# Weights of the first two combined Strassen items ranked ahead of the gate's taps, and no modulation step in them

## The chip, the core and the metric

The kernel runs on one core of a Trainium2 chip. The time is device microseconds of one execution, measured on the core. Three executions of the kernel before took 2934.47, 2937.22 and 2940.39 us, so the median is 2937.22 us. One more execution was profiled; all rows of the profile come from it.

## What is computed

Two layers, each a mixer and a convolutional feed-forward network (FFN), with a modulation of scales and shifts from a condition vector. Layer 0 mixes with a gated delta rule, layer 1 with retention. All in 32-bit floats, sequence 1024, model width 1024, FFN width 2816.

```python
e = silu(c @ cond_w + cond_b)
for i in range(2):
    mod = (e @ ada_w[i] + ada_b[i])[:, None, :]
    sh1, sc1, g1, sh2, sc2, g2 = split(mod, 6)
    y = mixers[i](x * (1.0 + sc1) + sh1)        # gated delta rule, then retention
    x = layer_norm(ALPHA * x + (1.0 + g1) * y, ln_g[i, 0], ln_b[i, 0])
    h = x * (1.0 + sc2) + sh2
    gate, up = split(h @ ffn_up[i], 2)
    gate = causal_dwconv(gate, conv_w[i]) + conv_b[i]   # 3 taps along the sequence
    y = (silu(gate) * up) @ ffn_down[i]
    x = layer_norm(ALPHA * x + (1.0 + g2) * y, ln_g[i, 1], ln_b[i, 1])
```

## The kernel before

**Products.** Every 32-bit operand of a matrix product is split into a high part, a rounded copy that ScalarE writes (line 89), and a low part, the difference that VectorE writes (line 90). `mm3` (lines 110 to 112) issues three matmuls for each pair: weights low by data high, high by low, high by high. The low part can only be made once the high part is there, and the first matmul of a triple needs the low part, so a product starts after its VectorE split.

**The Strassen stage.** `strassen` (from line 1153) computes a product of the transposed activations with weight columns, in *items* of two weight tiles each. It is called three times: for the up projection of the FFN of layer 0 (22 items), for the input projection of retention, and for the FFN of layer 1 (22 items). Items 0 and 1 are done plainly by `side`. From item 2 on an item is *combined*: `wino` does seven half-size products instead of eight, with four weight blocks a11, a12, a21, a22 (one DMA each for a11/a12 and a21/a22). Three of the products need sums of weight blocks, made on VectorE by `psub` (line 1205): s1 = a21 + a22, s2 = s1 - a11, s4 = a12 - s2, s3 = a11 - a21. Each product's weights are split by `block` into a tile `wb`. The products run in this order on TensorE: a11, a12, s1 by T1 (into Z), s2 by T2, s4 by 22, s3 by T3, a22 by T4. The T operands are sums of blocks of activations; `rest()`, called after the first plain item, issues what is left of them. A copy `pc` (line 1225, ScalarE) takes Z out after the product of s1.

In an FFN every even item is a gate item and every odd one the matching half of the up projection. A gate item ends in `conv()`: for each of four tiles one scaled copy on ScalarE (line 1579), two shifted multiply-adds ("taps") on VectorE (line 1584), a SiLU on ScalarE (line 1585). An up item multiplies the gate into it (line 1598), adds blocks on GpSimd (line 1605) and stores the result `o` to memory `ad` (line 1589).

**Modulation steps.** Parts of the modulation are computed bit by bit in the background. `bg` is a list of *units*; `bg_step()` runs the next one. A unit loads 512 KB of `ada_w` (tile `mvw`, line 216, on SyncE's queue) and adds it up in two VectorE instructions (lines 221 and 223, both 223 from the second unit of a group on); every fourth unit ends a group with four transposes on TensorE (line 233), four ScalarE copies (line 235) and a small addition. `wino` takes two steps in each combined item. The FFN of layer 0 has 40 units for its 20 combined items, so its list is empty when the stage ends; the FFN of layer 1 has 8 units; retention has none. While the stage runs, `mvw` tiles come from a spare tag; after it, `bg_tag` is "wr" (line 1265).

**The projection.** `proj_gen` does the down projection after each FFN, also by seven combined products. For layer 0 each product has 11 inner blocks of 12 matmuls. A block's two operands are `ab` (from a raw tile `ar`, read back from `ad`) and `bb` (from `Bw` or `Br`, `ffn_down`); both are split as above. `ab` tiles come in turn from the tags "wl", "hTb" and "wr" (block n from the n mod 3rd), and "wr" has two buffers. Each block calls `bg_step()` once (line 1503), which does nothing if the list is empty:

```python
at = ... ("wl", "hTb", "wr")[n % 3] if early else ...
a = two(at, F32R, "ab")
split(a[0], a[1], ra)
```

**What sets the order.** Each engine runs its instructions in the order of a list. A scheduler writes the lists ahead of time from the program's order as priority and from its own estimates of when operands are there; `tc.high_priority(n)` moves what is issued in it n places up in priority, and `tc.cur_priority` is the place now. A tag's buffers go round, so a tile waits until the last reader of the tile that had its buffer is done. SyncE's queue holds nearly all DMA issues and also runs in order: an issue that waits for a buffer holds all behind it.

Of the kernel before, what the change touches and what calls it, by code (L numbers as in the profile page):

```python
# [12 lines left out]
ALU = mybir.AluOpType  # L13
# [20 lines left out]
def trunk_kernel(ctx: ExitStack, tc, A):  # L34
    nc = tc.nc
    pe, act, dve, pool, sp = nc.tensor, nc.scalar, nc.vector, nc.gpsimd, nc.sync
# [9 lines left out]
    def tl(tag, shape, dt=F32, name=None):  # L46
        return sb.tile(shape, dt, tag=tag, name=name or tag, bufs=BUFS[tag])
# [40 lines left out]
    def split(dst_h, dst_l, src, eng=dve):  # L88
        act.activation(dst_h, src, AF.Copy)  # L89
        eng.tensor_tensor(dst_l, src, dst_h, ALU.subtract)  # L90
# [28 lines left out]
    def bg_step(tile=mm_tile):  # L119
        bg_ps[0] = tile  # L120
        if bg:
            bg.pop(0)()
# [38 lines left out]
    for k in range(KT):  # L161
        w = two("hTa", F32, "mvw")
# [617 lines left out]
    def t_solve(qd_):  # L780
        yield after_ev(("T0", 2 * qd_ - 1), ("A", 2 * qd_), ("A", 2 * qd_ + 1))
        yield from take("lane", 1)
        busy.append(qd_)
        X = tl("lane", [P, 32, 32], name="X")
        for h in pairs[2 * qd_] + pairs[2 * qd_ + 1]:
            for b in range(4):
                bs = slice(32 * b, 32 * b + 32)
                act.activation(X[bs, :, h % 4 * 8:h % 4 * 8 + 8].rearrange("p i c -> p c i"), U[h][bs, :, bs], AF.Copy)
        yield from take("lane", 2)
        yield LAT["X"]  # L790
        Y = tl("lane", [P, 32, 32], name="Y")
        dve.transpose(flat(Y), flat(X))
        T = tl("lane", [P, 32, 32], name="T")
# [210 lines left out]
    def tail(p, h, q4):  # L1004
# [3 lines left out]
        act.activation(d, o, AF.Square)  # L1008
        dve.tensor_reduce(so, d, AX.X, ALU.add)
        dve.scalar_tensor_tensor(so, so, 1.0 / P, ssq[h][:, qs], ALU.mult, ALU.add)  # L1010
# [82 lines left out]

    LAT = {"kk": 3.05, "ld": 1.14, "g1": 17.30, "gm": 2.50, "mm": 1.81, "T": 4.98, "X": 3.38, "fs": 2.2, "T0": 5.00, "t1": 1.65, "t2": 2.35, "t3": 1.34, "D": 2.67, "s1": 1.60, "s2": 1.22, "s3": 1.26, "tail": 12.31, "ssq": 9.30, "fv": 2.85}
    pairs = [(2 * p, 2 * p + 1) for p in range(GH // 2)]
# [57 lines left out]
    def strassen(hT0, xts, scale, shift, items, tags=("hTb", "hTb", "qkv", "qkv", "aux"), direct=False, beside=None, spare="lane"):  # L1153
        B = {"11": hT0[:4], "21": hT0[4:]}
        nblk = [0]
        nacc = [0]

        def mm_on(*a, **kw):
            return pe.matmul(*a, skip_group_check=True, **kw)  # L1159

        def side(n, s):
            out = []
            for u in items[n][:2]:
                w = load_w(u)
                X = acc_tile()
                for i, b in enumerate((("11", "21"), ("12", "22"))[s]):
                    for k in range(4):
                        mm3(X, w, k + 4 * i, B[b][k], i == 0 and k == 0, i == 1 and k == 3)
                out.append(X)
            return out  # L1170

        ahead, sinks = [], []
        for n in range(2):
            X = side(n, 0)
            if direct:
                sinks.append(items[n][2]())
                for i in range(2):
                    sinks[n](2 * i, X[i], None)
                continue
            ahead.append([tl("cv", [P, 516], name="ah")[:, 0:HALF] for _ in range(2)])  # L1180
            for t, x in zip(ahead[n], X):
                act.activation(t, x, AF.Copy)
        rest = build_T(B, xts, scale, shift, tags)

        def block(src):
            n = nblk[0]
            nblk[0] += 1
            t = tl(("wh", "wl")[n % 2], [P, 2, HALF], F32R, name="wb")
            split(t[:, 0], t[:, 1], src)
            return kn(t[:, 0]), kn(t[:, 1])  # L1190

        def prod(src, b, onto=None):
            w = block(src)
            if onto is None:
                nacc[0] += 1
                acc = (acc_tile, acc_tile, sc_tile)[nacc[0] % 3]()
            else:
                acc = onto
            for k in range(4):
                mm3(acc, w, k, B[b][k], onto is None and k == 0, k == 3, mm_on if onto is not None else pe.matmul)  # L1200
            return acc

        def psub(x, y, op=ALU.subtract):
            t = mm_tile()
            dve.tensor_tensor(t, x, y, op)  # L1205
            return t

        def wino(n, sink):
            ua, ub = items[n][:2]
            raws = []  # L1210
            for m, u in ((2 * n, ua), (2 * n + 1, ub)):
                if direct and m % 3 == 0:
                    raws += [tl("xT", [P, HALF], name="wr") for _ in range(2)]
                    for h2 in range(2):
                        anchor["i"] = sp.dma_start(raws[-2 + h2], u[:, hs(h2)])
                else:
                    w = tl("wr", [P, D])
                    anchor["i"] = sp.dma_start(w, u)
                    raws += [w[:, hs(0)], w[:, hs(1)]]
            if beside:  # L1220
                beside(n)
            a11, a12, a21, a22 = raws
            def copy_of(X, tag="cv"):
                t = tl(tag, [P, 516] if tag == "cv" else [P, HALF], name="pc")[:, 0:HALF]
                act.activation(t, X, AF.Copy)  # L1225
                return t

            X = prod(a11, "11")
            p1 = copy_of(X)
            s1 = psub(a21, a22, ALU.add)  # L1230
            sink(0, prod(a12, "21"), p1)
            s2 = psub(s1, a11)
            Z = prod(s1, "T1")
            z5 = copy_of(Z)
            s4 = psub(a12, s2)
            prod(s2, "T2", X)
            u2 = copy_of(X)
            s3 = psub(a11, a21)
            prod(s4, "22", Z)
            sink(1, Z, u2)  # L1240
            bg_step()
            prod(s3, "T3", X)
            u3 = copy_of(X, "t2")
            sink(3, X, z5)
            sink(2, prod(a22, "T4"), u3)
            bg_step()

        bg_tag[0] = spare
        for n in range(2):
            if not direct:  # L1250
                sinks.append(items[n][2]())
                for i in range(2):
                    sinks[n](2 * i, ahead[n][i], None)
            X = side(n, 1)
            for i in range(2):
                sinks[n](2 * i + 1, X[i], None)
            if n == 0:
                rest()
            if items[n][3]:
                items[n][3]()  # L1260
        for n in range(2, len(items)):
            wino(n, items[n][2]())
            if items[n][3]:
                items[n][3]()
        bg_tag[0] = "wr"
        return B
# [449 lines left out]
    for t in range(4):  # L1716
        if t % 2 == 0:
            xw = tl("lane", [P, 2, HALF], name="xlo")
        x = xw[:, t % 2]
# [273 lines left out]
```

## Time and profile before

| what | value |
|---|---|
| median of three executions | 2937.22 us (2934.47 to 2940.39) |
| the profiled execution | 2931.49 us |
| its span, first to last instruction | 2929.3 us |
| mean granted TensorE clock | 0.989 of full |
| TensorE busy | 2808.1 us (96%), 13638 matmuls |
| VectorE busy | 2198.4 us (75%) |
| ScalarE busy | 1316.2 us (45%) |
| GpSimd busy | 421.1 us (14%) |

Rows of a timeline read: start in us, duration in us, engine, line, operation, output<-inputs, tile shapes, how many; in brackets the idle time before it and what ended it. A row "xN" stands for N instructions one after the other. The duration of a matmul includes the time in which the next one is already running: at the full clock one starts every 0.227 us. Line numbers in rows are those of the kernel before.

### The profile page before, as it was taken

What the parts mean: (1) busy time and instruction counts of PE and PEld (TensorE: products, weight loads), DVE (VectorE), ACT (ScalarE), POOL (GpSimd) and SP (SyncE); (2) the same over time, 40 slices, a digit from 0 to 9 for tenths busy, and PEclk for the clock granted to TensorE, in tenths of its full rate; (3) what the DMA queues carried; (4) which work ended last, traced back from release to release, by engine and by line L of the source; (5) the groups of instructions that cost most, each with busy time, mean ns of one, the idle gap of its engine ahead of it and who ended that gap; (6) DMA issues with size and microseconds to landing.
All of it is one profiled execution on the core that took longest, in us unless ns stands there. A gap on an engine that the chain in (4) does not pass through costs nothing. (4 is left out here: it accounts for less than half of the span.)

```text
span 2929.3 us, 38823 instructions
## 1 busy us (share of the span) xinstructions
PE 2808.1 (96%) x13638; PEld 2296.3 (78%) x13638; DVE 2198.4 (75%) x3965; ACT 1316.2 (45%) x2457; POOL 421.1 (14%) x485
## 2 busy tenths in 40 slices
PE   8998999999999999999999999999999899999997
PEld 7777877887778888887787877777778688888786
DVE  6695687556788888897687766666697887778888
ACT  3755465443544444536443332221345544444443
POOL 0311220134011111100000000223201011111001
PEclk9999999999999999999999999999999999999999
DMA  8122221354344444863434454555564233335753
GB/s 309 64 80 80 98 91 44 105 187 148 108 150 159 163 157 147 316 218 123 157 110 173 149 181 149 165 172 163 189 235 155 94 137 108 108 108 202 262 158 119
DMA packets 239234, 442.35 MB, mean 151 GB/s; under 512 B 22848, under 2 KB 76352, under 8 KB 239040
## 3 DMA queue, kind: packets, MB, share of 16 engines
q1 hardware_dynamic: 206832, 387.96, 39.4%
q10 hardware_dynamic: 29760, 43.00, 4.0%
q0 software_dynamic: 2448, 8.91, 0.8%
q8 instruction: 107, 1.75, 0.2%
q14 instruction: 87, 0.71, 0.1%
HBM read 331.26 MB, written 108.53 MB: 150 GB/s over the span
## 5 line engine op out<-in xcount | busy, mean ns | idle before, releaser
L1466 PE MATMUL acc<-bb,ab 128*128 128x512 f32 x1800 | 427.5, 393 | 6.5 <-DVE pa L1441 2.5
L1466 PEld LDWEIGHTS acc<-bb,ab 128*128 128x128 f32 x1800 | 338.0, 189 | 81.4 <-DVE bb L90 3.8
L630 PE MATMUL acc<-hT,wh 128*128 128x512 f32 x960 | 300.3, 394 | 0.0
L1605 POOL TENSOR_TENSOR o<-o 128x512 f32<-128x512 f32 x88 | 121.1, 1387 | 810.6 <-DVE o L1598 680.4
L89 ACT ACTIVATE ab<-ar 128x512 fp32r<-128x512 f32 x210 | 129.0, 624 | 184.2 <-PE acc L1466 93.3
L1159 PE MATMUL acc<-T,wb 128*128 128x512 f32 x840 | 204.2, 392 | 7.2 <-DVE wb L90 7.2
L630 PEld LDWEIGHTS acc<-hT,wh 128*128 128x128 f32 x960 | 183.0, 191 | 34.0
L630 PE MATMUL acc<-hT,wl 128*128 128x512 f32 x480 | 202.8, 422 | 0.8 <-DVE qkv L993 0.5
L1159 PEld LDWEIGHTS acc<-T,wb 128*128 128x128 f32 x840 | 157.9, 189 | 43.7 <-DVE wb L90 11.1
L90 DVE TENSOR_TENSOR ab<-ar,ab 128x512 fp32r<-128x512 f32 x210 | 146.4, 703 | 44.2 <-ACT ab L89 44.2
L90 DVE TENSOR_TENSOR wb<-mm,wb 128x512 fp32r<-128x512 f32 x216 | 145.2, 684 | 23.4 <-ACT wb L89 21.7
L90 DVE TENSOR_TENSOR wb<-wr,wb 128x512 fp32r<-128x512 f32 x162 | 111.3, 688 | 65.7 <-ACT wb L89 63.8
L1225 ACT ACTIVATE pc<-acc 128x512 f32<-128x512 f32 x143 | 84.7, 592 | 160.5 <-PE acc L1159 91.6
L89 ACT ACTIVATE wh<-wr 128x1024 fp32r<-128x1024 f32 x101 | 107.0, 1061 | 110.2 <-PE acc L630 50.3
L89 ACT ACTIVATE wb<-mm 128x512 fp32r<-128x512 f32 x216 | 122.3, 593 | 72.8 <-DVE mm L1205 72.1
L90 DVE TENSOR_TENSOR wl<-wr,wh 128x1024 fp32r<-128x1024 f32 x85 | 105.5, 1241 | 61.2 <-ACT wh L89 59.1
L89 ACT ACTIVATE wb<-wr 128x512 fp32r<-128x512 f32 x162 | 99.7, 627 | 96.5 <-DMA wr<-in_ffn_up 53.0
L449 DVE SCALAR_TENSOR_TENSOR qkv<-raw,vc,qkv 128x512 f32<-128x512 f32 x144 | 112.3, 783 | 34.8 <-ACT qkv L447 30.7
L630 PE MATMUL acc<-wh,hT 128*128 128x512 f32 x384 | 135.5, 415 | 0.7 <-DVE vv L90 0.7
L1584 DVE SCALAR_TENSOR_TENSOR o<-g,vc,o 128x512 f32<-128x512 f32 (+2 forms) x176 | 135.2, 786 | 0.7
L223 DVE SCALAR_TENSOR_TENSOR ada<-mvw,e,ada 128x512 f32<-128x512 f32 x140 | 105.9, 757 | 27.0 <-DMA mvw<-in_ada_w 26.5
L110 PE MATMUL acc<-T,wb 128*128 128x512 f32 x292 | 116.6, 399 | 9.9 <-DVE wb L90 9.4
(626 smaller groups left out, 6876.5 us busy)
## 6 DMA issues: line engine op xcount, KB each, us to landing
wr<-in_ffn_up SPq DMA_DIRECT2D x96, 512.0 KB, 4.3
ad<-o SPq DMA_DIRECT2D x154, 256.0 KB, 2.2
ar<-ad SPq DMA_DIRECT2D x154, 256.0 KB, 4.2
mvw<-in_ada_w SPq DMA_DIRECT2D x48, 512.0 KB, 5.5
Br<-in_ffn_down SPq DMA_DIRECT2D x66, 256.0 KB, 3.3
mvw<-in_ada_w SPq DMA_DIRECT2D x64, 256.0 KB, 3.0
wr<-in_ret_wv SPq DMA_DIRECT2D x32, 512.0 KB, 4.2
ar<-od SPq DMA_DIRECT2D x56, 256.0 KB, 5.0
```

Of the source, the lines that this page charges most:

```text
L89: act.activation(dst_h, src, AF.Copy)
L90: eng.tensor_tensor(dst_l, src, dst_h, ALU.subtract)
L110: mm(acc, wl[:, k], hl[0], start=first, stop=False)
L223: dve.scalar_tensor_tensor(a, wr[kk], e[:, k:k + 1], a, ALU.mult, ALU.add)
L449: dve.scalar_tensor_tensor(oh, raw[:, 3 - j:515 - j], w[:, 3 - j:4 - j], oh, ALU.mult, ALU.add)
L630: pq(pe.matmul(out, lhsT, rhs, start=start, stop=stop, **kw), cost)
L1159: return pe.matmul(*a, skip_group_check=True, **kw)
L1225: act.activation(t, X, AF.Copy)
L1466: mm_ = (lambda *a, p=p, onto=onto, **kw: (mm if p < 2 else pe.matmul)(*a, skip_group_check=onto, **kw))
L1584: dve.scalar_tensor_tensor(tv, gv[:, c0 - j:c1 - j], w[:, 2 - j:3 - j], tv, ALU.mult, ALU.add)
L1605: pool.tensor_tensor(o[d], o[x], o[y], op)
```

## The change

`strassen` notes the priority at the point behind `rest()` of the first plain item, ahead of that item's `conv()` (the list `mark`). In items 2 and 3, the first two combined ones, the sums of weights (`psub`) and the splits (`block`) are issued at the priority of that point, by the context manager `rank`. And these two items call no `bg_step()`. The number of units stays, so the four steps that are no longer taken there are taken later: in the FFN of layer 1 in items 4 to 7 instead of 2 to 5; in the FFN of layer 0, where 40 units stood against 40 steps, the last four units are left when the stage ends, and the projection's first product takes them, one at each of its blocks 0 to 3.

```diff
--- before.py
+++ after.py
@@ -1154,6 +1154,7 @@
         B = {"11": hT0[:4], "21": hT0[4:]}
         nblk = [0]
         nacc = [0]
+        mark = []
 
         def mm_on(*a, **kw):
             return pe.matmul(*a, skip_group_check=True, **kw)
@@ -1182,15 +1183,19 @@
                 act.activation(t, x, AF.Copy)
         rest = build_T(B, xts, scale, shift, tags)
 
-        def block(src):
+        def rank(n):
+            return tc.high_priority(tc.cur_priority - mark[0]) if n < 4 else nullcontext()
+
+        def block(src, it):
             n = nblk[0]
             nblk[0] += 1
             t = tl(("wh", "wl")[n % 2], [P, 2, HALF], F32R, name="wb")
-            split(t[:, 0], t[:, 1], src)
+            with rank(it):
+                split(t[:, 0], t[:, 1], src)
             return kn(t[:, 0]), kn(t[:, 1])
 
-        def prod(src, b, onto=None):
-            w = block(src)
+        def prod(it, src, b, onto=None):
+            w = block(src, it)
             if onto is None:
                 nacc[0] += 1
                 acc = (acc_tile, acc_tile, sc_tile)[nacc[0] % 3]()
@@ -1200,9 +1205,10 @@
                 mm3(acc, w, k, B[b][k], onto is None and k == 0, k == 3, mm_on if onto is not None else pe.matmul)
             return acc
 
-        def psub(x, y, op=ALU.subtract):
+        def psub(it, x, y, op=ALU.subtract):
             t = mm_tile()
-            dve.tensor_tensor(t, x, y, op)
+            with rank(it):
+                dve.tensor_tensor(t, x, y, op)
             return t
 
         def wino(n, sink):
@@ -1225,25 +1231,27 @@
                 act.activation(t, X, AF.Copy)
                 return t
 
-            X = prod(a11, "11")
+            X = prod(n, a11, "11")
             p1 = copy_of(X)
-            s1 = psub(a21, a22, ALU.add)
-            sink(0, prod(a12, "21"), p1)
-            s2 = psub(s1, a11)
-            Z = prod(s1, "T1")
+            s1 = psub(n, a21, a22, ALU.add)
+            sink(0, prod(n, a12, "21"), p1)
+            s2 = psub(n, s1, a11)
+            Z = prod(n, s1, "T1")
             z5 = copy_of(Z)
-            s4 = psub(a12, s2)
-            prod(s2, "T2", X)
+            s4 = psub(n, a12, s2)
+            prod(n, s2, "T2", X)
             u2 = copy_of(X)
-            s3 = psub(a11, a21)
-            prod(s4, "22", Z)
+            s3 = psub(n, a11, a21)
+            prod(n, s4, "22", Z)
             sink(1, Z, u2)
-            bg_step()
-            prod(s3, "T3", X)
+            if n > 3:
+                bg_step()
+            prod(n, s3, "T3", X)
             u3 = copy_of(X, "t2")
             sink(3, X, z5)
-            sink(2, prod(a22, "T4"), u3)
-            bg_step()
+            sink(2, prod(n, a22, "T4"), u3)
+            if n > 3:
+                bg_step()
 
         bg_tag[0] = spare
         for n in range(2):
@@ -1256,6 +1264,7 @@
                 sinks[n](2 * i + 1, X[i], None)
             if n == 0:
                 rest()
+                mark.append(tc.cur_priority)
             if items[n][3]:
                 items[n][3]()
         for n in range(2, len(items)):
```

The lists of the engines change in these places. In all rows below numbers behind a name tell tiles apart; the lines of the changed kernel are some 6 to 9 higher (1211 is `psub`, 1588, 1593 and 1594 are `conv`, 1607 the multiplication, 1231 the copy `pc`, 1280 the load of `ar`, 1313 of `Bw` and `Br`, 1598 the store, 1367 the load of `xg`, 1369 its additions).

VectorE, first combined item of the FFN of layer 0, before. `wb_7443` is the split of s1, `wb_7463` of s2, `wb_7482` of s4, `mm_7461` is s4:

```order
L1570 TENSOR_TENSOR g_7398<-sc_7427,pc_7420 128x512
L1584 SCALAR_TENSOR_TENSOR o_7306<-g_7137,vc_153,o_7306 128x512
L1584 SCALAR_TENSOR_TENSOR o_7301<-g_7137,vc_153,o_7301 128x510
L1584 SCALAR_TENSOR_TENSOR o_7311<-g_7138,vc_153,o_7311 128x511
L1584 SCALAR_TENSOR_TENSOR o_7316<-g_7138,vc_153,o_7316 128x512
L1584 SCALAR_TENSOR_TENSOR o_7306<-g_7137,vc_153,o_7306 128x512
L90 TENSOR_TENSOR wb_7443<-mm_7422,wb_7443 128x512
L221 TENSOR_SCALAR ada_7498<-mvw_7499,e_162 128x512
L1584 SCALAR_TENSOR_TENSOR o_7542<-g_7398,vc_153,o_7542 128x511
L1584 SCALAR_TENSOR_TENSOR o_7311<-g_7138,vc_153,o_7311 128x510
L1598 TENSOR_TENSOR o_7301<-o_7301,ah_7053 128x512
L1584 SCALAR_TENSOR_TENSOR o_7316<-g_7138,vc_153,o_7316 128x512
```

The same place in the changed kernel:

```order
L90 TENSOR_TENSOR T4_7298<-bt_7129,T4_7297 128x512
L1593 SCALAR_TENSOR_TENSOR o_7301<-g_7137,vc_153,o_7301 128x511
L1579 TENSOR_TENSOR g_7398<-sc_7427,pc_7420 128x512
L1593 SCALAR_TENSOR_TENSOR o_7306<-g_7137,vc_153,o_7306 128x512
L1593 SCALAR_TENSOR_TENSOR o_7301<-g_7137,vc_153,o_7301 128x510
L90 TENSOR_TENSOR wb_7443<-mm_7422,wb_7443 128x512
L1593 SCALAR_TENSOR_TENSOR o_7311<-g_7138,vc_153,o_7311 128x511
L1593 SCALAR_TENSOR_TENSOR o_7306<-g_7137,vc_153,o_7306 128x512
L1593 SCALAR_TENSOR_TENSOR o_7316<-g_7138,vc_153,o_7316 128x512
L1593 SCALAR_TENSOR_TENSOR o_7533<-g_7398,vc_153,o_7533 128x511
L1211 TENSOR_TENSOR mm_7461<-wr_7400,mm_7441 128x512
```

Between the row that makes g_7398 and the split of s1 stand two taps where five stood, and the two modulation instructions on ada_7498 are gone; the split of s2, wb_7463, now comes 11 rows behind that of s1, where it came 12 behind. Then ScalarE, which makes the high parts of the same tiles, before:

```order
L1579 ACTIVATE o_7306<-g_7137,vc_153 128x512
L1579 ACTIVATE o_7311<-g_7138,vc_153 128x512
L1579 ACTIVATE o_7316<-g_7138,vc_153 128x512
L89 ACTIVATE wb_7443<-mm_7422 128x512
L1579 ACTIVATE o_7542<-g_7398,vc_153 128x512
L1585 ACTIVATE o_7301<-o_7301,vc_153 128x512
L1585 ACTIVATE o_7306<-o_7306,vc_153 128x512
L1585 ACTIVATE o_7311<-o_7311,vc_153 128x512
L1585 ACTIVATE o_7316<-o_7316,vc_153 128x512
L89 ACTIVATE wb_7463<-mm_7441 128x512
L89 ACTIVATE wb_7482<-mm_7461 128x512
L1225 ACTIVATE pc_7459<-acc_7446 128x512
```

And in the changed kernel:

```order
L1588 ACTIVATE o_7301<-g_7137,vc_153 128x512
L1588 ACTIVATE o_7306<-g_7137,vc_153 128x512
L89 ACTIVATE wb_7443<-mm_7422 128x512
L1588 ACTIVATE o_7311<-g_7138,vc_153 128x512
L1588 ACTIVATE o_7316<-g_7138,vc_153 128x512
L1588 ACTIVATE o_7533<-g_7398,vc_153 128x512
L1594 ACTIVATE o_7301<-o_7301,vc_153 128x512
L1594 ACTIVATE o_7306<-o_7306,vc_153 128x512
L1231 ACTIVATE pc_7459<-acc_7446 128x512
L89 ACTIVATE wb_7463<-mm_7441 128x512
L89 ACTIVATE wb_7482<-mm_7461 128x512
```

The high part of s1 moves ahead of two scaled copies. The high parts of s2 and s4, which stood ahead of `pc_7459`, the copy of the product of s1, now stand behind it.

The third place is the start of the down projection of layer 0. On SyncE's queue ar_11115 loads the raw tile of inner block 16, the sixth of the second product. Before:

```order
L1271 DMA ar_11115<-ad0_6924 128x512
L1304 DMA Br_11123<-in_ffn_down 128x512
L1271 DMA ar_11144<-ad0_6924 128x512
L1589 DMA ad0_6924<-o_10528 128x512
L1304 DMA Br_11152<-in_ffn_down 128x512
L1589 DMA ad0_6924<-o_10518 128x512
L1589 DMA ad0_6924<-o_10523 128x512
L1358 DMA xg_10846<-xs0_66 128x512
L1589 DMA ad0_6924<-o_10513 128x512
```

In the changed kernel:

```order
L1280 DMA ar_11115<-ad0_6924 128x512
L216 DMA mvw_10760<-in_ada_w 128x2x512
L1598 DMA ad0_6924<-o_10499 128x512
L1598 DMA ad0_6924<-o_10494 128x512
L1313 DMA Br_11123<-in_ffn_down 128x512
L1598 DMA ad0_6924<-o_10489 128x512
L1598 DMA ad0_6924<-o_10484 128x512
L1280 DMA ar_11144<-ad0_6924 128x512
L1313 DMA Br_11152<-in_ffn_down 128x512
L216 DMA mvw_10791<-in_ada_w 128x2x512
L1280 DMA ar_11166<-ad0_6924 128x512
```

Here are two of the four loads of the units that moved, mvw_10760 and mvw_10791; mvw_10730 stands some 30 rows higher, ahead of the raw tile of block 4, and mvw_10821 seven rows below mvw_10791. On VectorE at this place ab_10838 is the split of block 5's `ab` tile, ab_11044 that of block 13. Before:

```order
L1360 TENSOR_TENSOR xg_10766<-xg_10766,rowb_10708 128x512
L90 TENSOR_TENSOR bb_10788<-Bw_10715,bb_10788 128x512
L90 TENSOR_TENSOR ab_10838<-ar_10836,ab_10838 128x512
L1360 TENSOR_TENSOR xg_10793<-xg_10793,rowb_10708 128x512
L1360 TENSOR_TENSOR xg_10819<-xg_10819,rowb_10708 128x512
L90 TENSOR_TENSOR ab_10865<-ar_10863,ab_10865 128x512
L90 TENSOR_TENSOR bb_10868<-Bw_10791,bb_10868 128x512
L1598 TENSOR_TENSOR o_10528<-o_10528,sc_10540 128x512
```

In the changed kernel:

```order
L90 TENSOR_TENSOR bb_10948<-Bw_10844,bb_10948 128x512
L90 TENSOR_TENSOR bb_10980<-Br_10924,bb_10980 128x512
L90 TENSOR_TENSOR ab_11044<-ar_11042,ab_11044 128x512
L223 SCALAR_TENSOR_TENSOR ada_10729<-mvw_10760,e_162,ada_10729 128x512 x2
L223 SCALAR_TENSOR_TENSOR ada_10729<-mvw_10791,e_162,ada_10729 128x512 x2
L1369 TENSOR_TENSOR xg_10846<-xg_10846,rowb_10677 128x512
L90 TENSOR_TENSOR ab_10838<-ar_10836,ab_10838 128x512
L1369 TENSOR_TENSOR xg_10846<-xg_10846,rowb_10681 128x512
L1369 TENSOR_TENSOR xg_10872<-xg_10872,rowb_10677 128x512
```

The split of block 5 stood ahead of those of blocks 6 and 7; it now stands behind those of blocks 6, 7, 10, 9 and 13 and behind the second and third moved unit, and the two `wr` buffers take mvw and ab tiles in turn: ab_10838 gets the one that mvw_10791 had. On TensorE the blocks keep their order: 4, 5, 6.

## The prediction

> **What bounds the kernel now.** I read the page's busy times first, then what TensorE waited for, then the two stages that the change touches, and last the place where the dropped modulation steps go.
>
> ```profile
> PE 2808.1 (96%) x13638; PEld 2296.3 (78%) x13638; DVE 2198.4 (75%) x3965; ACT 1316.2 (45%) x2457; POOL 421.1 (14%) x485
> PE acc L110 <- DVE wb L90: 9.4, 2, 4.7
> PE acc L1159 <- DVE wb L90: 7.2, 8, 1.9
> ```
>
> TensorE is busy for 96% of the span, so an edit is worth what TensorE waits less or more. The largest wait in the list is the change's target: twice 4.7 us for a VectorE split (line 90) of a sum of weights. In TensorE's timeline this is the first combined item of the FFN of layer 0, at the product of s1:
>
> ```profile
> 800.26 0.39 PE L112 MATMUL sc<-hT,wb 128*128 128x512 f32 x1
> 805.34 0.79 PE L110 MATMUL acc<-T,wb 128*128 128x512 f32 x1 [4.69 <-DVE wb L90]
> 805.93 0.63 PE L111 MATMUL acc<-T,wb 128*128 128x512 f32 x1
> 810.20 0.55 PE L112 MATMUL acc<-T,wb 128*128 128x512 f32 x1
> 812.64 4.41 PE L1159 MATMUL acc<-T,wb 128*128 128x512 f32 x12 [1.89 <-DVE wb L90]
> 819.84 0.39 PE L110 MATMUL acc<-T,wb 128*128 128x512 f32 x1
> 800.00:805.00 5.00, 0.65 (x3) 0.19 (x1) 5.00 (x9) 3.80 (x7) 0.00 (x0) 0.87 0.00 0
> 805.00:810.00 5.00, 4.66 (x11) 3.69 (x12) 5.00 (x9) 2.85 (x5) 0.00 (x0) 0.50 0.14 54
> 815.00:820.00 5.00, 5.00 (x18) 3.97 (x18) 1.28 (x2) 1.20 (x2) 2.89 (x3) 0.77 0.65 193
> 2313.50 0.79 PE L110 MATMUL acc<-T,wb 128*128 128x512 f32 x1 [4.69 <-DVE wb L90]
> 2320.80 3.01 PE L1159 MATMUL acc<-T,wb 128*128 128x512 f32 x12 [1.82 <-DVE wb L90]
> 2326.36 0.39 PE L110 MATMUL acc<-T,wb 128*128 128x512 f32 x1
> ```
>
> Idle from 800.65 to 805.34, then 12 matmuls that start every 0.427 us, since the granted clock (third number from the right in the rows by stretch) has fallen to 0.50; then 1.89 us for the split of s2, and again some matmuls at half the clock (0.77 over 815 to 820). T4 starts at 819.84. The last three rows are the same item in the FFN of layer 1: the waits are the same, but its 12 matmuls of s2 take 3.01 us in place of 4.41, so no half clock followed there.
>
> VectorE and ScalarE at that place say why:
>
> ```profile
> 800.68 0.69 DVE L1570 TENSOR_TENSOR g<-sc,pc 128x512 f32<-128x512 f32 x1
> 801.29 3.39 DVE L1584 SCALAR_TENSOR_TENSOR o<-g,vc,o 128x512 f32<-128x512 f32 x5
> 804.60 0.69 DVE L90 TENSOR_TENSOR wb<-mm,wb 128x512 fp32r<-128x512 f32 x1
> 809.37 0.74 DVE L223 SCALAR_TENSOR_TENSOR ada<-mvw,e,ada 128x512 f32<-128x512 f32 x1
> 811.90 1.28 DVE L90 TENSOR_TENSOR wb<-mm,wb 128x512 fp32r<-128x512 f32 x2
> 801.64 0.58 ACT L89 ACTIVATE wb<-mm 128x512 fp32r<-128x512 f32 x1
> 810.78 0.60 ACT L1225 ACTIVATE pc<-acc 128x512 f32<-128x512 f32 x1 [0.79 <-PE acc L112]
> ```
>
> VectorE is never idle there. Its split of s1 waits behind five taps (3.39 us), not for its high part, which ScalarE has at 802.2.
>
> **The rank, FFN of layer 0.** In the new order two taps stand ahead of that split, not five. Three taps at 0.66 us (3.39 over five, less the overlap) come out: the split runs at 802.6 and the product of s1 starts at about 803.35, a wait of 2.70 us in place of 4.69. That is still 79% idle of the clock's window before 803.69, so I keep half the clock behind it: the product ends at about 807.8. For s2 the new VectorE list has seven taps, the sum s4 and two multiplications between the two splits (7 x 0.66 + 3 x 0.60 us), and no modulation: the split of s2 comes at 809.6 instead of 811.90. Its ScalarE half now stands behind the copy `pc`, which waits for the end of the product of s1: done at about 808.9, just in time. The product of s2 starts at 810.35 after 2.6 us idle; with half the clock again T4 starts at 817.5. Gain **2.3 us**; with the full clock behind s2 it would be 4.0.
>
> **The rank, FFN of layer 1.** The same starts, but less to win back, since the clock was full behind s2: **1.5 us**, between 0.7 (half the clock behind s2 now) and 2.4 (full). Two smaller waits can go:
>
> ```profile
> 2340.89 2.34 PE L1159 MATMUL sc<-T,wb 128*128 128x512 f32 x9 [0.76 <-DVE wb L90]
> 1500.37 1.88 PE L1159 MATMUL sc<-T,wb 128*128 128x512 f32 x7 [0.61 <-DVE wb L90]
> ```
>
> The first is item 3's split of s2 in the FFN of layer 1, which stands behind a modulation instruction that moves away; the second is in item 3 of retention. I count **0.8 and 0.5**, and 0 as the other end. The gains add up to 5.1 us, between 3 and 9.
>
> **The four steps that leave the stage of layer 0.** They come back in the projection's first product, and they are no longer beside slack. Before:
>
> ```profile
> 1197.76 7.55 PE L1466 MATMUL acc<-bb,ab 128*128 128x512 f32 x32
> 1205.50 52.88 PE L1466 MATMUL acc<-bb,ab 128*128 128x512 f32 x232
> 1262.86 1.43 PE L1466 MATMUL sc<-bb,ab 128*128 128x512 f32 x5 [1.76 <-DVE ab L90]
> 1200.00:1210.00 10.00, 10.00 (x48) 8.26 (x47) 10.00 (x18) 4.57 (x14) 0.00 (x0) 1.00 1.05 388
> 1210.00:1220.00 10.00, 10.00 (x46) 8.28 (x45) 10.00 (x17) 6.37 (x15) 3.90 (x2) 1.00 1.05 398
> ```
>
> TensorE runs there without a wait for 63 us, but VectorE is full (10.00 of 10.00) and so are the DMA engines (share 1.05, 388 GB/s). The unit's load is 512 KB, its additions two VectorE instructions. Were that all, 8 x 0.66 us of VectorE and 2 MB of transfer would cost little. What decides is the order. Block 5 of the first product takes its `ab` tile from "wr", and "wr" has two buffers that the moved `mvw` tiles now share. In the new lists the split of block 5 stands behind both additions of the third unit, on VectorE and through its buffer; that unit's load stands on SyncE behind the raw tile of block 16. TensorE takes block 5 in its old place, and nothing behind it can pass.
>
> When block 5 is due: 60 matmuls come ahead of it, 32 from 1197.76 and 28 from 1205.50 at 52.88/232 = 0.228 us, so 1211.9. When its operand is there, on the clock of the run before:
>
> ```profile
> 1192.94 0.32 SPq L1271 DMA_DIRECT2D ar<-ad  x1
> ...
> 1210.27 0.32 SPq L1271 DMA_DIRECT2D ar<-ad  x1
> 1211.72 0.33 SPq L1304 DMA_DIRECT2D Br<-in_ffn_down  x1
> 1213.58 0.32 SPq L1271 DMA_DIRECT2D ar<-ad  x1
> ...
> 1192.09 0.68 DVE L90 TENSOR_TENSOR bb<-Bw,bb 128x512 fp32r<-128x512 f32 x1
> 1206.70 0.68 DVE L90 TENSOR_TENSOR ab<-ar,ab 128x512 fp32r<-128x512 f32 x1
> 1213.22 1.25 DVE L239 TENSOR_TENSOR v<-cs,vc 128x4 f32<-128x4 f32 x1
> mvw<-in_ada_w SPq DMA_DIRECT2D x48, 512.0 KB, 5.5
> ```
>
> - SyncE issued the raw tile of block 4 at 1192.94 and that of block 16 at 1210.27, 25 issues of mostly 256 KB later: 0.69 us each, the pace of 385 GB/s. The first unit's load goes ahead of block 4 (two such slots, 1.4 us), so block 16's is issued at 1211.6, the second unit's at 1212.3, and after its two slots and seven more issues the third unit's at 1218.5.
> - VectorE must have finished the first unit before that load may take its buffer. From the first `bb` split at 1192.09 to the row at 1213.22 there are 34 instructions, 0.62 us each. The first unit's second addition is the 38th: done at 1216.2, so the queue decides.
> - The load lands 5.5 us after its issue (row of the DMA issues): 1224.0. Then two additions (1.4 us), the ScalarE half (0.63) and the VectorE half of the split (0.68), with an addition on `xg` ahead of it whose load is issued three places behind the unit's (1221.2, landing at 1226.5): split done at about 1227.8, where it was done at 1207.4 before.
>
> TensorE waits **16 us** at block 5. Bounds: had the load gone out when VectorE let it (1216.2) and no `xg` been in the way, 12.5; with SyncE held for 2 us more by the stores among those seven issues (the row at 1213.58 was held 1.9 us after the one ahead), 18. The fourth unit's load, seven issues behind the third's, lands at about 1229.6, and block 8, which needs its buffer, is due only at 1236: no second wait. Behind the wait comes half the clock: in the row at 805.93, 12 matmuls lost 0.2 us each, **2.4 us**. The Trainium skill (TensorE: Matmul & The Clock Gate, "The HAM clock gate") has it that after an idle window the next 3.4 us or so run at half rate, which would make this 1.7 us by an estimate from that page; the sum would be 0.7 us less. Given back is the wait of 1.76 us at 1262.86, since VectorE is far ahead of TensorE by then: **-1.8**. Loss 16.6 us, between 11 and 21.
>
> **Sum.** 16.6 - 5.1 = 11.5 us slower: 2943.0 us against the profiled execution's 2931.49. The three runs have their median 5.7 us higher, at 2937.22, so I predict 2948.7, rounded to **2948.5**.
>
> **Rivals.**
> - *No wait in the projection.* If the loads land early enough, as they would were SyncE not paced by full DMA engines, only the gains stay: 2937.2 - 5.1 = 2932.1. Against it: even the bound by VectorE alone puts block 5 at 1224. Chance 0.12.
> - *The stages give all they lost.* If the split of s1 comes soon enough that the clock never falls, T4 of layer 0 starts near 809: 11 us there and 9.4 in layer 1, 20.4 in all with 16.6 lost: 2933.4. This is the side that ends faster, where the wait at block 5 is also nearer 12.5: 2929. For it: the clock is half of the cost. Against it: the list still has three taps ahead, and the clock fell after 1.89 us idle as well (815 to 820). Chance 0.10.
> - *The stages give nothing.* If ScalarE's half of s2, now behind `pc`, comes later than I have it, TensorE starts s2 near 812.6 as before: no gain, 2937.2 + 16.6 = 2953.8. For it: the margin is under 1 us. Chance 0.13.
> - *More of the wait is given back.* The blocks behind block 5 are ready early. Beside the 1.76 us counted, TensorE waited in this line for `bb` splits:
>
> ```profile
> PE acc L1466 <- DVE bb L90: 1.8, 3, 1.1
> ```
>
> If these vanish too: 2948.5 - 1.8 = 2946.7. Chance 0.05.
>
> **Chances.** The forecast has 0.60. Its own range is 2942 to 2954. A measurement of this kernel tells 0.2%, 5.9 us, from no change: faster is below 2931.3, slower above 2943.1. Faster 0.09 (half of the second rival, a third of the first), the same 0.23 (the rest of these two, and 0.10 of the forecast, its low end), slower 0.68. The range that should hold it 8 times in 10 reaches to the first two rivals: 2932 to 2956.
>
> **What would show it.** In the profile after: a first row of block 5 in the down projection of layer 0, some 14 us into it, with 12 to 18 us idle before it, ended by VectorE's `ab` split, and a `mvw` load as what VectorE waited for; a granted clock of 0.5 just behind; waits of about 2.7 and 2.6 us at s1 and s2 where 4.69 and 1.89 stood. Block 5 without a wait would make the forecast wrong by its whole sign, and full clock through 800 to 820 would make the gains too small.

## The result, and the profile after

The changed kernel takes 2951.83 us (median of six executions, 2949.55 to 2954.20), the kernel before 2936.23 in as many. The medians differ by 15.6 us, where 11.5 were forecast. The ratio on record is 1.0044, with a 95% interval of 1.0033 to 1.0055, which is 12.9 us (9.7 to 16.1); it need not be the quotient of the two medians, here and in the runs below, but the sign is the same by both. Ratios leave out the one execution in a slow state, which the run called "other buffer" below had (4702.75 us at a granted clock of 0.557).

What TensorE waited for, in the changed kernel (total us, times, longest; the first, third and sixth rows of the list):

```profile
PE acc L1475 <- DVE ab L90: 19.3, 1, 19.3
...
PE acc L1160 <- DVE wb L90: 8.0, 7, 2.4
...
PE acc L110 <- DVE wb L90: 5.4, 2, 2.7
```

The head of the list has a new line: one wait of 19.3 us in the projection (line 1475), for a split of `ab`. The wait that the change was aimed at (line 110) has gone from 9.4 us to 5.4.

TensorE's timeline at the three places, first combined item of the FFN of layer 0, start of its projection, first combined item of layer 1:

```profile
807.30 0.79 PE L110 MATMUL acc<-T,wb 128*128 128x512 f32 x1 [2.70 <-DVE wb L90]
814.33 4.51 PE L1160 MATMUL acc<-T,wb 128*128 128x512 f32 x12 [2.42 <-DVE wb L90]
821.41 0.39 PE L110 MATMUL acc<-T,wb 128*128 128x512 f32 x1
...
1197.31 6.06 PE L1475 MATMUL acc<-bb,ab 128*128 128x512 f32 x26
1203.56 8.00 PE L1475 MATMUL acc<-bb,ab 128*128 128x512 f32 x34
1230.82 8.38 PE L1475 MATMUL acc<-bb,ab 128*128 128x512 f32 x29 [19.26 <-DVE ab L90]
1283.76 1.66 PE L1475 MATMUL sc<-bb,ab 128*128 128x512 f32 x6 [1.69 <-DVE ab L90]
...
2332.31 0.50 PE L110 MATMUL acc<-T,wb 128*128 128x512 f32 x1 [2.71 <-DVE wb L90]
2339.34 4.60 PE L1160 MATMUL acc<-T,wb 128*128 128x512 f32 x12 [2.42 <-DVE wb L90]
2346.54 0.39 PE L110 MATMUL acc<-T,wb 128*128 128x512 f32 x1
```

After 26 + 34 = 60 matmuls, five blocks, TensorE stands at block 5. SyncE and VectorE in the meantime:

```profile
1212.16 0.32 SPq L1280 DMA_DIRECT2D ar<-ad  x1
1213.52 0.38 SPq L216 DMA_DIRECT2D mvw<-in_ada_w  x1
1216.99 1.48 SPq L1598 DMA_DIRECT2D ad<-o  x2
1220.03 0.32 SPq L1280 DMA_DIRECT2D ar<-ad  x1
1221.20 0.38 SPq L216 DMA_DIRECT2D mvw<-in_ada_w  x1
...
1216.44 0.75 DVE L223 SCALAR_TENSOR_TENSOR ada<-mvw,e,ada 128x512 f32<-128x512 f32 x1
1227.00 1.54 DVE L223 SCALAR_TENSOR_TENSOR ada<-mvw,e,ada 128x512 f32<-128x512 f32 x2 [4.00 <-DMA mvw<-in_ada_w]
1229.47 0.69 DVE L1369 TENSOR_TENSOR xg<-xg,rowb 128x512 f32<-128x512 f32 x1 [0.94 <-DMA xg<-xs]
1230.08 0.68 DVE L90 TENSOR_TENSOR ab<-ar,ab 128x512 fp32r<-128x512 f32 x1
```

This is the chain of the prediction link by link: raw tile of block 16, load of the second unit, the stores, a raw tile that is held until 1220.03, load of the third unit at 1221.20; its additions at 1227.00; an addition on `xg`, for whose load VectorE waits another 0.94 us; the split of block 5. By stretches (us, then busy time of TensorE, its weight loads, VectorE, ScalarE, GpSimd; granted clock; DMA share; GB/s):

```profile
1210.00:1220.00 10.00, 1.56 (x7) 0.94 (x6) 7.37 (x14) 5.00 (x9) 0.07 (x1) 0.68 1.05 392
1220.00:1230.00 10.00, 0.00 (x0) 0.00 (x0) 5.00 (x7) 0.63 (x1) 3.38 (x2) 0.50 0.98 350
1230.00:1240.00 10.00, 9.18 (x36) 7.46 (x37) 8.98 (x15) 2.15 (x4) 0.00 (x0) 0.80 1.07 389
```

TensorE does nothing for a whole stretch in which before it was never idle, and VectorE, whose work it waits for, is idle half of that stretch: what runs all the time is DMA.

Seven landmarks in TensorE's timeline split each profiled execution: the end of the matmul ahead of the wait for s1, the first matmul of T4 in that item, the first of the projection, the first of the next stage that reads its operand tile `12` (line 110, `acc<-12`), and in the FFN of layer 1 the same first three. The differences, in us, for all kernels that follow too (in those called "late" the calls for the left units are late; the work is not, as told there):

| kernel | first item, layer 0 | rest of its stage | projection, layer 0 | first item, layer 1 | rest of its stage |
|---|---|---|---|---|---|
| before | 19.19 | 377.92 | 244.67 | 17.55 | 370.06 |
| the change | 16.81 | 375.90 | 265.85 | 16.94 | 370.30 |
| rank only | 18.92 | 378.83 | 246.42 | 19.02 | 370.33 |
| steps only | 16.50 | 375.95 | 265.25 | 16.49 | 369.12 |
| list emptied | 16.89 | 383.58 | 244.53 | 16.75 | 373.38 |
| other buffer | 16.90 | 376.23 | 250.28 | 16.93 | 369.92 |
| late, no rank | 16.51 | 376.96 | 250.41 | 16.50 | 369.09 |
| late, rank | 16.92 | 375.37 | 249.31 | 16.93 | 369.41 |
| late, both splits, rank | 13.78 | 376.77 | 248.48 | 13.19 | 370.10 |
| late, both splits, no rank | 15.32 | 375.97 | 249.32 | 15.05 | 369.72 |
| both splits, rank, all steps | 14.18 | 378.96 | 244.67 | 14.27 | 373.08 |
| the same, steps dropped in layer 1 alone | 14.19 | 378.49 | 244.31 | 13.17 | 371.12 |

In the change the stage of layer 0 is 4.4 us shorter and the projection 21.2 longer. The profiled execution of the change is 21.1 us longer in span than that of before, more than the 15.6 of the medians: 3.95 us of it lie ahead of the first landmark (800.65 before, 804.60 after). They are there at 780 us already, ahead of the first place where the engines' lists differ: the dropped load of a unit, which SyncE issued at 784.86 in the kernel before. That part is told of at the end.

### The profile page after: what moved, and what is told of

It is laid out like the page before. It is cut to its first block, busy times and chain, and to the rows that moved or that the text cites. A ratio compares the mean times of both kernels' runs of the same rounds, so it can differ in the third digit from the quotient of the medians.

```text
span 2950.4 us, 38833 instructions
## 1 busy us (share of the span) xinstructions
PE 2814.1 (95%) x13638; PEld 2302.1 (78%) x13638; DVE 2200.7 (75%) x3965; ACT 1317.5 (45%) x2457; POOL 417.8 (14%) x485
## 4 chain that ended last, share of the span: by engine, by line
PE 67%; DVE 13%; DMA 7%; issue 7%; ACT 4%; POOL 1%; SPq 0%; ACTq 0%; DVEq 0%; POOLq 0%
PE acc L630 15%; PE acc L1160 8%; PE acc L1475 8%; PE acc L110 4%; PE acc L111 4%; PE acc L112 4%; PE sc L1160 4%; PE sc L630 4%; PE sc L1475 3%; PE mm L630 2%; DMA mvw<-in_ada_w 2%; PE sc L110 2%; PE sc L111 2%; PE sc L112 2%; PE mm L633 1%
## 5 line engine op out<-in xcount | busy, mean ns | idle before, releaser
L1475 PE MATMUL acc<-bb,ab 128*128 128x512 f32 x1800 | 428.4, 394 | 25.2 <-DVE ab L90 19.3
L1160 PE MATMUL acc<-T,wb 128*128 128x512 f32 x840 | 205.9, 395 | 8.1 <-DVE wb L90 8.0
L1160 PEld LDWEIGHTS acc<-T,wb 128*128 128x128 f32 x840 | 159.3, 190 | 44.8 <-DVE wb L90 11.5
L1211 DVE TENSOR_TENSOR mm<-wr 128x512 f32<-128x512 f32 x108 | 78.2, 724 | 59.8 <-DMA wr<-in_ffn_up 35.1
```

Source lines behind the costliest of these rows:

```text
L1475: mm_ = (lambda *a, p=p, onto=onto, **kw: (mm if p < 2 else pe.matmul)(*a, skip_group_check=onto, **kw))
```

## Experiments

**Which part costs: the rank or the steps.** Theory A: block 5 waits because its buffer goes round behind the moved units. B: the moved units' work is too much for a full stretch. C: the rank costs.

Rank only, the steps taken in all items:

```diff
-            if n > 3:
-                bg_step()
+            bg_step()
```

> The rank is kept, the two modulation steps are taken in items 2 and 3 as before, so no unit is left for the projection. Theory A (block 5 of layer 0's down projection waits because its buffer goes round behind the moved units): only the gains stay, 4 to 7 us less than before's 2936, so about 2930; waits of about 2.7 us at s1 in both FFNs, no wait over 2 us in the first 60 us of the projection. Theory B (the loss is the moved units' work, 8 VectorE instructions and 2 MB, in a stretch where VectorE and DMA are full): the same 2930. Theory C (the rank itself costs, by the ScalarE halves that now stand behind the copy of the product of s1): about 2950.

2936.72 us, ratio 0.9990 (0.9981 to 0.9999). Nothing is left of the loss, so C falls. But the gain is 2 us, not 4 to 7, with an interval that only just leaves out none; the profiled execution shows no gain at all (its five stretches of the table are together 4.1 us longer than before). The first item shows why:

```profile
809.41 0.79 PE L110 MATMUL acc<-T,wb 128*128 128x512 f32 x1 [2.71 <-DVE wb L90]
817.50 2.93 PE L1160 MATMUL acc<-T,wb 128*128 128x512 f32 x6 [3.55 <-DVE wb L90]
```

The wait at s1 falls from 4.69 to 2.71 us and the wait at s2 grows from 1.89 to 3.55. The taps that the split of s1 no longer waits for now stand ahead of the split of s2, with two modulation instructions; VectorE is never idle between the two splits:

```profile
808.67 0.69 DVE L90 TENSOR_TENSOR wb<-mm,wb 128x512 fp32r<-128x512 f32 x1
816.76 1.28 DVE L90 TENSOR_TENSOR wb<-mm,wb 128x512 fp32r<-128x512 f32 x2
814.49 1.08 ACT L89 ACTIVATE wb<-mm 128x512 fp32r<-128x512 f32 x2
```

The item takes 18.92 us where it took 19.19, and in layer 1, where half the clock now follows s2 as well, 19.02 where it took 17.55.

Steps only, without the rank:

```diff
-            return tc.high_priority(tc.cur_priority - mark[0]) if n < 4 else nullcontext()
+            return nullcontext()
```

> No rank; only the steps are dropped in items 2 and 3. Theory A and B: the loss without the gains: a wait of about 19 us at block 5, about 2955 (2936 + 19 + 2 for half the clock, less 1 to 2 for the modulation instructions gone from the two items). Theory C: about 2935, within 3 us of before.

2949.84 us, ratio 1.0033 (1.0020 to 1.0045).

```profile
805.74 0.80 PE L110 MATMUL acc<-T,wb 128*128 128x512 f32 x1 [4.69 <-DVE wb L90]
811.98 3.02 PE L1160 MATMUL acc<-T,wb 128*128 128x512 f32 x12 [1.15 <-DVE wb L90]
1225.83 9.56 PE L1475 MATMUL acc<-bb,ab 128*128 128x512 f32 x32 [18.07 <-DVE ab L90]
```

The whole loss is here without the rank, and so is the whole gain in the stages: 16.50 and 16.49 us for the first items, a little better than with the rank. The wait at s1 is the full 4.69 us; the wait at s2 falls to 1.15, and no half clock follows it (12 matmuls in 3.02 us, where the kernel before took 4.41).

**The buffer or the work.** The change, with the four left units in the tag "xT", which block 5's operand doesn't use (it has two buffers of half a unit each, so a load becomes two of 256 KB); all eight additions stay in the projection's first two products, and so do six of the eight loads; the scheduler placed the first two far ahead, at 533.78 and 536.12:

```diff
-        bg_tag[0] = "wr"
+        bg_tag[0] = "xT"
         return B
```

> The change, with the four left units still in the projection's first product, but their tiles in a tag of their own (two half tiles, so two DMAs of 256 KB each) instead of the one that block 5's operand shares. The work and the bytes moved in are the same. Theory A: the wait at block 5 falls from 19.3 us to under 2 us; about 2930 to 2932. Theory B: a wait of over 10 us somewhere in the first 60 us of the projection remains; about 2945 to 2952.

2937.30 us, ratio 0.9994 (0.9983 to 1.0004), against 1.0044 for the change. The wait at block 5 is gone: TensorE runs 225 matmuls without a stop through the place. A wait of 4.40 us stands at the third product instead, where the kernel before waited 1.76:

```profile
1204.15 51.30 PE L1475 MATMUL acc<-bb,ab 128*128 128x512 f32 x225
1264.65 1.19 PE L1475 MATMUL sc<-bb,ab 128*128 128x512 f32 x2 [4.40 <-DVE ab L90]
```

So A accounts for some 16 of the projection's 21.2 us, and 5.6 us remain. The wait is 2.6 us longer than before's, and behind it the throttle's record has half the clock until about 1270.5, 5.9 us after the restart, in which half the work is lost: 2.9 us. The granted clock is 0.68 from 1260 to 1270, where it was 1.00 before. What came late for that wait is the raw tile of the third product:

```profile
1246.28 0.73 DVE L223 SCALAR_TENSOR_TENSOR ada<-mvw,e,ada 128x512 f32<-128x512 f32 x1
1251.16 0.73 DVE L223 SCALAR_TENSOR_TENSOR ada<-mvw,e,ada 128x512 f32<-128x512 f32 x1
1255.43 1.27 DVE L1377 TENSOR_TENSOR xt<-xt,rowb 128x512 f32<-128x512 f32 x2
1247.05 5.21 SPq L1221 DMA_DIRECT2D wr<-in_ret_wg  x2
1254.33 0.93 SPq L1661 DMA_DIRECT2D sinT<-in_sinT  x2
1257.12 0.42 SPq L1280 DMA_DIRECT2D ar<-ad  x1
1263.15 0.63 ACT L89 ACTIVATE ab<-ar 128x512 fp32r<-128x512 f32 x1 [6.08 <-DMA ar<-ad]
```

In the kernel before, that raw tile was issued at 1253.01:

```profile
1244.64 7.92 DVE L1368 TENSOR_TENSOR xt<-xt,rowb 128x512 f32<-128x512 f32 x13
1248.37 1.54 SPq L1652 DMA_DIRECT2D sinT<-in_sinT  x2
1253.01 0.38 SPq L1271 DMA_DIRECT2D ar<-ad  x1
```

In both kernels the raw tile goes out some 0.4 us behind the last of sixteen VectorE additions on `xt` (line 1377, 1368 before), because the loads ahead of it on SyncE's queue, of `sinT` and `gb`, wait for those additions. Counted from the projection's first matmul, the last addition ends after 54.8 us before and after 60.2 here. Eight additions of the units stand ahead of it, and VectorE had little slack to take them: up to that point, from 5 us ahead of the first matmul, it was busy for 55.1 of 59.8 us before and is for 61.8 of 65.2 here. Two loads for the next stage stand in the queue as well (`wr<-in_ret_wg`, issued from 531.53 on in the kernel before; they take "xT" too and wait here for the units' last additions), but they are out by 1252.3, and what comes behind them waits for `xt` all the same. So the 5.6 us are theory B in a small size, as far as the trace tells; no run takes the additions out and leaves the loads.

**Units kept in the stage.** The change, with the two left steps per item given to items 4 to 7, so that none is left over:

```diff
-            if n > 3:
-                bg_step()
+            for _ in range(0 if n < 4 else 2 if n < 8 else 1):
+                bg_step()
```

> The change, with one step more in each of the items 4 to 7, so that the 40 units are done when the stage of layer 0 ends. Theory A and B: no wait at block 5, about 2930, 4 to 7 us faster than before. If the extra units make VectorE late in items 4 to 7 instead, waits of up to 1 us each there and 2933. Theory C: about 2950.

2942.97 us, ratio 1.0021 (1.0011 to 1.0032): slower than before, where even the worse case that I named was 2933. The projection is as before (244.53), but the rest of the stage takes 383.58, and 3.74 us of it are one wait for the split of s1 in a later item:

```profile
913.69 0.80 PE L110 MATMUL sc<-T,wb 128*128 128x512 f32 x1 [3.74 <-DVE wb L90]
```

with 6.8 us of half the clock in the throttle's record from 913.1 on. The FFN of layer 1, where the eight units now also come three to an item, has such a wait too (3.34 us at 2426.57), and its rest of the stage takes 373.38. In the 9 us ahead of the late split VectorE has four instructions of the units; three steps in an item, two of them together at its end, are too many here.

**The left units late.** Next, the units in the tag "xT" and called only from the projection's fourth product on (`p > 2`), without and with the rank:

```diff
-                bg_step()
+                if not gain or p > 2:
+                    bg_step()
```

> No rank; the steps are dropped in items 2 and 3; the four left units wait for the projection's fourth and later products and have their own tag. By the stages of the runs so far: first combined item 2.7 us shorter in layer 0 and 1.1 in layer 1, the rest of both stages 2.0 and 0.9 shorter, the projection within 1.5 us of before. In all about 6 us faster than before (ratio 0.998). If the units cost their VectorE time wherever they stand, the projection keeps some 5 us of loss as it did with the other tag, and the time is the same as before.

2934.39 us, ratio 0.9990 (0.9981 to 1.0000).

> The same with the rank, so the whole change with its left units made harmless. If the rank only moves the wait from the split of s1 to that of s2 (as the run with the rank alone looks), this is within 1 us of the run without it. If the rank gains 2 us in each FFN on top, it is 4 us faster than that one.

2936.84 us, ratio 0.9998 (0.9989 to 1.0007). The first is 3 us faster than before, half of what I expected, the second not faster at all, since the projection still takes 249 to 250 us: the wait at the third product stays (4.84 and 3.75 us). The edit moved the calls and not the work. In the run without the rank the units' first and last additions are these:

```profile
1211.37 0.47 DVE L221 TENSOR_SCALAR ada<-mvw,e 128x512 f32<-128x512 f32 x1
1249.21 0.74 DVE L223 SCALAR_TENSOR_TENSOR ada<-mvw,e,ada 128x512 f32<-128x512 f32 x1
```

They stand 16.6 and 54.5 us behind the projection's first matmul, as in the run with the other buffer (16.4 and 54.6), ahead of the third product. The scheduler placed loads and additions as early as there, and only the end of the group (transposes and copies) comes some us later. So these runs don't tell what late units would cost, and it is no wonder that the few us stay. Between the two the intervals overlap; the rank shows no gain over the dropped steps. Its two waits in the first item are again 2.70 and 2.60:

```profile
807.01 0.50 PE L110 MATMUL acc<-T,wb 128*128 128x512 f32 x1 [2.70 <-DVE wb L90]
814.03 4.62 PE L1160 MATMUL acc<-T,wb 128*128 128x512 f32 x12 [2.60 <-DVE wb L90]
```

**What keeps s2 late.** If the rank only moves the wait on, the split of s2 must come ahead of the taps together with that of s1. This stands on top of the last edits, again with and without the rank:

```diff
+            w1 = w2 = None
+            if n < 4:
+                w1 = block(s1, n)
+                w2 = block(s2, n)
-            Z = prod(n, s1, "T1")
+            Z = prod(n, s1, "T1", w=w1)
             ...
-            prod(n, s2, "T2", X)
+            prod(n, s2, "T2", X, w=w2)
```

> The same with the rank, and in items 2 and 3 the split of s2 is issued ahead of the product of s1, right behind the split of s1. If what keeps s2 late is its place behind the taps and behind the copy of the product of s1, its wait of 2.4 us goes and with it the second stretch at half the clock: first combined item about 13 us from the end of the product before to T4, in place of 16.8; 10 to 13 us faster than before. If the split of s4 becomes the next late one, 15 us and 7 us faster.

2925.94 us, ratio 0.9960 (0.9947 to 0.9973).

```profile
809.49 0.50 PE L110 MATMUL acc<-T,wb 128*128 128x512 f32 x1 [2.70 <-DVE wb L90]
813.91 2.93 PE L1160 MATMUL acc<-T,wb 128*128 128x512 f32 x12
817.72 0.96 PE L1160 MATMUL acc<-22_7074,wb 128*128 128x512 f32 x3 [0.88 <-DVE wb L90]
```

The product of s2 follows without a wait; the split of s4 is next late, by 0.88 us. The first items take 13.78 and 13.19 us.

> As the last, without the rank: the wait at s1 stays 4.7 us with half the clock behind it, the one at s2 goes: first combined item about 15.8 us, 7 us faster than before. The rank's own worth, with s2 out of the way, is the difference to the run with it: about 2.5 us in each FFN.

2930.98 us, ratio 0.9980 (0.9970 to 0.9989): first items of 15.32 and 15.05 us, with 4.69 us of wait at s1 and none at s2. With s2 out of the way the rank is worth 1.5 and 1.9 us in the two items, where I expected about 2.5 in each.

**Without touching the steps.** Last, rank and both splits with the steps back in items 2 and 3, in both FFNs (shown) and in that of layer 0 alone; tag and calls in the projection are as in the kernel before:

```diff
-            if n > 3:
-                bg_step()
+            bg_step()
```

> Rank, and the splits of s1 and s2 together ahead of the product of s1 in items 2 and 3, with all modulation steps taken there as in the kernel before, so the projection is as before. If the projection's remaining 4 to 5 us (a wait of 4.0 us at 1265 in the run with the late units, where before had 1.76, and half the clock behind it) come from the left units, the projection takes 244.7 us again; the modulation instructions make the split of s4 up to 1.3 us later in each first combined item, and the rest of the stage of layer 0 takes 378 again. In all about 2926, within 2 us of the run with the late units.

2926.91 us, ratio 0.9965 (0.9953 to 0.9977). The projection takes 244.67 us again, to the hundredth as before: with no unit left over, nothing of the loss is left.

> The same, with the steps dropped in items 2 and 3 of the FFN of layer 1 alone, where its 8 units only move to items 4 to 7. If that frees the split of s4 there without a new wait, 1 to 2 us faster than the last, about 2925; if items 4 to 7 pay for it, the same as the last.

2926.35 us, ratio 0.9962 (0.9948 to 0.9976). In this last run the first item and the rest of the stage of layer 1 are together 3.1 us shorter than in the one ahead, which the medians don't show. No difference between the three kernels with both splits and the rank, at 10 to 12 us less than the kernel before, can be told. The plainest is the one with all steps where they were: the two splits together, with the rank.

## Why the prediction was right, and where it was not

The time (2948.5 against 2951.83), the sign and the cause are as forecast. Step by step, with the steps' own numbers:

- *The wait at block 5*: 16 us forecast, 19.26 measured. The mechanism is shown by the run with the other tag, in which it vanishes with the additions and three quarters of the loads still there. The size was off on SyncE: the third unit's load went out at 1221.20 and not at 1218.5. The queue was held longest ahead of the raw tile at 1220.03, where the profile names the landing of the second unit's load as what ended the wait (1.5 us); I had named the stores there as the upper bound, 2 us more, and taken none of it. The load took 5.8 us to its additions in place of 5.5, and in the end the load of `xg` decided: it went out at 1222.98 in place of 1221.2, and its addition began 6.5 us later in place of 5.3. The bound of 18 us was too low by 1.3.
- *Half the clock behind it*: 2.4 us forecast. The record has half the clock until about 1234.0, 3.2 us after the restart, in which half the work is lost: 1.6 us. The Trainium skill's 3.4 us at half rate (TensorE: Matmul & The Clock Gate, "The HAM clock gate"), 1.7 us by my estimate from that page, was nearer than the row that I took.
- *Given back, 1.8 us*: wrong. The wait at the third product is there as before, 1.69 us at 1283.76. VectorE did run ahead, as I took it to, but that doesn't help: in its list the splits of the third product stand behind the multiplications of the second product's results (line 1434), and the first of these waits for TensorE to finish that product:

```profile
1275.31 0.69 DVE L1434 TENSOR_TENSOR c<-acc,rowb 128x512 f32<-128x512 f32 x1 [10.28 <-PE acc L1475]
1283.02 0.69 DVE L90 TENSOR_TENSOR ab<-ar,ab 128x512 fp32r<-128x512 f32 x1
```

- *The projection as a whole* takes 21.2 us more, where 16.6 were forecast: the wait, the half clock and the 1.8 us that were not given back.
- *The rank, FFN of layer 0, 2.3 us*: the item is 2.4 us shorter, and the waits of 2.70 and 2.42 us are nearly the 2.7 and 2.6 forecast. But the step's ground failed. I put the gain down to the rank; the run with the rank alone gains 0.3 us, the one with the steps alone 2.7. The rank takes 2 us off the wait at s1 and gives most of them to the wait at s2; what makes the item shorter is that two modulation instructions are gone from ahead of the split of s2. The number came right because the sum was worked out from the new list, in which both edits are at work, and only the name over it was wrong.
- *FFN of layer 1, 1.5 us*: 0.6 measured, just below the lower bound of 0.7; half the clock did follow s2 (12 matmuls in 4.60 us).
- *The two smaller waits, 0.8 and 0.5 us*: both are gone, and nothing is gained. The rest of layer 1's stage is no shorter (370.30 against 370.06): its units now stand in items 4 to 7, and a wait of 0.84 us came up at 2424.59, behind a unit's load for which VectorE waited 3.35 us. From the fourth landmark to the fifth, retention among it, the two kernels differ by less than 0.1 us (866.4).
- *Not foreseen*: the rest of layer 0's stage is 2.0 us shorter, with or without the rank (375.90 and 375.95 against 377.92). Four units fewer run in it; with all steps back it takes 378.5 to 379.0.

The gains in the two FFNs come to 4.8 us, near the 5.1 forecast, but that is luck in part: 2.0 us of them were not foreseen, and they fill in for what the FFN of layer 1 and the two smaller waits did not give.

Of the rivals, the first (no wait), the second (half the clock stayed behind s1 and s2) and the fourth (the `bb` waits are still 1.5 us in all) fell. The third, that the stages give nothing, is nearest to the truth for the rank alone, though not by its mechanism. It had ScalarE's half of s2 come late; in the run with the rank alone that half is begun at 814.49, and it is VectorE, never idle, that comes to its split of s2 only at 816.76.

## What to carry to other kernels

Work that is dropped from one place of a list comes out at another: look there first, at what it shares a buffer with and what stands ahead of it in the in-order queue that loads it. Here a tile from a two-buffer tag that a background task also drew from made one matmul wait 19.3 us for the task's transfers, though the task was four loads and eight additions. In a tag without that operand the same additions still cost 5.6 us. A call that stands later in the program need not run later: look in the trace where the scheduler put it. And when a split is moved ahead of other work on its engine, move the next one of the same chain with it, or, as here, the wait may only move one product on.

## What the runs showed that was not expected

Executions differ by several us in a part that no edit touches. In the seven kernels that keep "wr" as the tag of the left units, the engines' lists are the same up to 784 us. Yet their first landmark, some 800 us into the program, lies between 800.65 (before) and 806.71 us (rank only), and nearly all of the difference is there at 780 us already. The throttle's record shows stretches of half the clock of 3.41 or 6.83 us that begin at other waits of this part in each execution, 24 to 41 us in all ahead of the landmark. Their sum alone does not explain the difference: it is 30.7 us in the profiled execution of the kernel before and in that of the change, which are 3.95 us apart. The cause stays open. So a difference of 3 us between two profiled executions says nothing by itself here; the landmarks inside one execution do.
